# A decoder block on one core: ten up-projection pairs begun early, and down passes opened by four tiles with row buffers of their own

## The chip, the cores and the metric

The kernel runs on one core of one Trainium2 chip. The time is device microseconds (us) of one execution. Five engines matter here. TensorE (PE in the profile) multiplies matrices. VectorE (DVE) and ScalarE (ACT) do element-wise work. GpSimd (POOL) and SyncE (SP) do hardly anything here but issue transfers between the memory of the chip and the on-chip buffers. On ACT, DVE, POOL and SP the instructions of this trace start in the order of the engine's queue, so an instruction that waits holds up everything behind it on that engine, and a transfer that waits for its buffer holds up the transfers behind it in the same issuing queue.

## The reference

What is computed is one decoder block of 2048 channels over 512 tokens in float32. The first half (input projection, an RWKV-7 mixer, a pooling mixer) is not touched. The change lies in what follows it:

```python
mix = jnp.concatenate([y_rwkv, y_pool], axis=-1) @ w_out[l]      # 2048 -> 2048
x = x + gt1 * mix
h = _rmsnorm(x, norm2_g[l]) * (1.0 + sc2) + sh2
x = x + gt2 * _conv_ffn(h, w_up[l], conv_w[l], conv_b[l], w_down[l])
...
return _rmsnorm(x, norm_f_g)
```

`_conv_ffn` multiplies by `w_up` (2048 to 2 x 5632 columns, values and gates), convolves each column causally over three tokens, takes silu(gate) x value and multiplies by `w_down` (5632 to 2048). The two norms run over the 2048 channels of each token, so nothing of a token's second norm can be known before all sixteen output tiles of 128 channels have their values for that token.

## The kernel before

**Layout.** Channels lie on the 128 partitions, tokens along the free dimension. A tile `f` (0 to 15) is 128 channels by 512 tokens; `H0` and `H1` are the first and the second 256 tokens. Each float32 operand is split in a rounded part and a rest (`hi`, `lo`), and each product is three matmuls (`mm3`, L119 to L123). For weights ACT makes the rounded part (the cast of L837, or L114 in the output projection) and DVE the rest (L839, L116). The split weights have three buffers of each kind.

**Output projection** (L693 to L806). Tiles 0 to 7 are accumulated together in eight banks, tiles 8 and 9 (`NW = 10`) one after the other over all tokens, and tiles 10 to 15 first for `H0`, then for `H1`, as half tiles. `residual` (L734) adds a finished tile to `x` on DVE (L737), squares it on ACT (L731, into `sqx`) and adds the square to `acc` on DVE (L732). `out_done` stores the new `x` tile from SP (L764). During the last four half tiles the `H0` half is normed (`normed`, L779: one DVE multiply and four ACT instructions per four tiles) and split (`split4`, L786).

**Up projection.** The product with `w_up` is computed per pair j (0 to 43) of a value and a gate tile. It is one step of the Strassen-Winograd scheme: the tokens are cut in `H0` and `H1`, the channels in two halves, and each pair takes seven half-size products instead of eight. The operands on the side of `x` are Y11, Y21 (halves of `H0`) and T1 to T4, Y22 (sums that need `H1` as well). A product (`product`, L842) is 24 matmuls with 256 columns. The two rows of `w_up` of a pair (1 MB each) are loaded by SP (L852) into four buffers `x2_0` to `x2_3`, the ones that held `x` before; GpSimd adds to them in the transfer (L948 for r1, L951 for r3); DVE makes r2 and r4 (L972, L979). r2, r3, r4 and all other wide scratch, `sqx` among it, share one ring of three buffers, `wide` (L710).

The first two products of a pair need only `H0`. `first_two` (L859) makes them for `NB = 5` pairs before the loop and holds the sums in five of ten scratch buffers (`Slot`, L821; a list from which the longest free one is taken). Meanwhile `combos` (L871) norms the `H1` half and makes and splits T1 to T4 and Y22, one of four large steps after each pair. The loop over pairs (L941) then has five products for the first five pairs and seven for the other 39. The last product of pair j (`last_product`, L929) is issued in the iteration of pair j+1, and `finish_pair` (L914) convolves, multiplies and stores the result `ad` from SP (L924).

**Down projection** (L1008 to L1093). The 44 rows of `ad` are taken in two passes of 22. `act_pair` (L1008) loads them back through slots (`al`) and splits them. `down` (L1020) goes through one output tile in three blocks of up to eight rows, each with one weight transfer (L1024) into the `wide` ring. Pass one stores its sixteen partial tiles `yd` from SP (L1039). Pass two loads them and `x` (`load_x2`, L1054) from SP, adds tiles 0 to 7 over all tokens, then tiles 8 to 15 for `H0` and for `H1`, each followed by `residual`. The final norm of `H0` is written out (`finish`, L1068) between the last half tiles, that of `H1` at the end.

**Order.** Apart from a few marked places ahead of the change, no order is written by hand. A planner of the framework fixes each engine's queue before the run: the order of the program is the priority, and an instruction whose operands or whose buffer are not yet free by the planner's own estimates comes behind ready ones. Buffers of one ring are handed out in program order. At run time an instruction waits for its own operands and its own buffer, but never overtakes.

Of the kernel before, what the change touches and what calls it, by code (L numbers as in the profile page):

```python
# [9 lines left out]
F32 = mybir.dt.float32  # L10
# [6 lines left out]
P = 128  # L17
T = 512
D = 2048
KT = D // P  # L20
# [1 line left out]
NP = 8  # L22
NC = 4
WC = 512
NW = 10
NWF = 8
NSLOT = 10
NB = 5
NJ = NF // 2
Q = float(np.exp(-0.5))  # L30
WINS = (2, 4, 8, 16)
# [25 lines left out]
def block_kernel(ctx, tc, a, out, stop=None, dbg=None):  # L57
# [664 lines left out]
        return x2q[f // 4][:, f % 4, sl]  # L722

    acc = rb.tile([P, T], F32, tag="acc", name="acc")

    def sumsq(acc, src, lo, hi, fresh):
        if fresh:
            S.activation(acc[:, lo:hi], src, AF.Square)
        else:
            t = wide("sqx")[:, 0:2, :].rearrange("p a b -> p (a b)")  # L730
            S.activation(t[:, lo:hi], src, AF.Square)  # L731
            V.tensor_add(acc[:, lo:hi], acc[:, lo:hi], t[:, lo:hi])  # L732

    def residual(f, ps, gate, acc, lo, hi, fresh):  # L734

# [37 lines left out]
    def out_half(hf, f):  # L773
        ps = bank()[:, 0:HT]
# [41 lines left out]


    ub = ctx.enter_context(tc.tile_pool(name="ub", bufs=1, side="right", reuse_waits="tile"))
    free = [(ub, f"s{i}") for i in range(NSLOT)]

    class Slot:  # L821

# [31 lines left out]

    W1, W2 = slice(0, 2 * QW), slice(2 * QW, 4 * QW)
    T1, T2, T3, T4, Y22 = ([None, None] for _ in range(5))
    ahead = []

    def first_two(n):  # L859

        w = row(2 * n, ub, f"t4{n % 2}")
        s_ = Slot("u1")
        ps = bank()[:, 0:HT]
        product(ps, w[:, W1], Y11)
        S.copy(s_[:, H1], ps)
        ps = bank()[:, 0:HT]
        product(ps, w[:, W2], Y21)
        V.tensor_add(s_[:, H0], s_[:, H1], ps)
        ahead.append(s_)

    def combos(step):  # L871
        if step in (0, 1):
            normed(step, H1, rstd)
            t = wide("t1")
            V.tensor_sub(t, x2q[step][:, :, H0], x2q[step][:, :, H1])
            T1[step] = split4(ub, f"t1{step}", t)
        elif step in (2, 3):
            g = step - 2
            normed(g + 2, H1, rstd)
            t3 = wide("t3")  # L880
            V.tensor_sub(t3, x2q[g + 2][:, :, H1], x2q[g][:, :, H1])
            t2 = wide("t2")
            V.scalar_tensor_tensor(t2, t3, -1.0, x2q[g][:, :, H0], op0=ALU.mult, op1=ALU.subtract)
            T2[g] = split4(ub, f"t2{g}", t2)
            T3[g] = split4(ub, f"t3{g}", t3)
            Y22[g] = split4(ub, f"y22{g}", x2q[g + 2][:, :, H1])
# [3 lines left out]
    t4 = []  # L890
# [23 lines left out]
    def finish_pair(j, u1, u2):  # L914
        yv, yg = Slot("yv"), Slot("yg")
        conv(u1.t, yv.t, col("cw", j), col("cw", 88 + j), col("cw", 176 + j), col("cb", j))
        u1.done()

        conv(u2.t, yg.t, ncw[:, 0, j : j + 1], ncw[:, 1, j : j + 1], ncw[:, 2, j : j + 1], col("cb", 44 + j))
        u2.done()  # L920
        S.activation(yg.t, yg.t, AF.Silu)
        V.tensor_mul(yv.t, yv.t, yg.t)
        yg.done()
        nc.sync.dma_start(ad[j], yv.t)  # L924
        yv.done()

    pend = None
# [13 lines left out]
    for j in range(NF):  # L941
        w = []
        for i in range(2):
            w.append(row(2 * j + i, rb, f"x2_{rows % 4}"))
            rows += 1

        w11, w12, r1, w22 = w[0][:, W1], w[0][:, W2], w[1][:, W1], w[1][:, W2]
        G.dma_start(r1, a["wup"][2 * j + 1, :, W2], accum_op=ALU.add)  # L948
# [3 lines left out]
        early = j < NB  # L952
        pa = bank()[:, 0:HT]
        cap = Slot("cap")
        if early:
            u1 = ahead[j]
            if pend:
                last_product(pend)
        else:
            product(pa, w11, Y11)  # L960
            S.copy(cap[:, H0], pa)
            last_product(pend)
            u1 = Slot("u1")
            pb = bank()[:, 0:HT]
            product(pb, w12, Y21)
            V.tensor_add(u1[:, H0], cap[:, H0], pb)
# [3 lines left out]
        S.copy(cap[:, H1], pc)  # L970
        r2 = wide("r2").rearrange("p a b -> p (a b)")
        V.tensor_add(r2, r1, w11)  # L972
        product(pa, r2, T2, start=early)
        if early:
            V.tensor_add(cap[:, H0], u1[:, H1], pa)
        else:
            S.copy(cap[:, H0], pa)
# [1 line left out]
        V.tensor_add(r4, r2, w12)  # L979
        product(pc, r4, Y22, start=False)  # L980
        V.tensor_add(u1[:, H1], cap[:, H0], pc)
        if early:
# [46 lines left out]

    yd = [tc.dram_tile([P, T], F32, name=f"yd{f}") for f in range(KT)]  # L1030
    A = []
    for i in range(NJ // 2):
        A += act_pair(i)
    for f in range(KT):
        ps = bank()
        down(ps, f, 0, A)
        s_ = Slot("yd")
        S.copy(s_.t, ps)
# [13 lines left out]
    x2q = [quad(i, "x2") for i in range(4)]  # L1052

    def load_x2(f):  # L1054
        nc.sync.dma_start(x2(f), x2d[f])
        s_ = Slot("yd")
        nc.sync.dma_start(s_.t, yd[f])
        V.scalar_tensor_tensor(x2(f), s_.t, gate(f), x2(f), op0=ALU.mult, op1=ALU.add)
        s_.done()

# [10 lines left out]
        nc.sync.dma_start(out[:, k, hs], x2(k, hs))  # L1071

    for f in range(NWF):
        load_x2(f)
        load_x2(f + NWF)
        ps = bank()
        down(ps, f, 1, A)
        residual(f, ps, gate(f), acc, 0, T, f == 0)
    for f in range(NWF, KT):
        down_half(0, f)  # L1080
# [111 lines left out]
```

## Time and profile before

| | |
|---|---|
| median of 3 runs | 2539.76 us (2536.63 to 2545.37) |
| the profiled execution | 2535.93 us, of which the span is 2534.2 us |
| PE busy in the span | 2319.7 us (92%) |
| DVE, ACT, POOL busy | 1639.3, 1038.2, 78.8 us |
| mean granted TensorE clock | 0.974 |
| transfers | 470.44 MB, mean 186 GB/s |

The page divides the span in 40 slices of 63.4 us. The output projection lies in slices 13 to 16 (781 to 975 us), the early products and the pair loop from there to slice 31 (1915 us), pass one of the down projection to 2167 us and pass two to 2519 us. Transfers reach up to 365 GB/s in 10 us stretches. In the timelines of an engine a row is the start in us, the duration, the engine, the line, the operation, its result and operands, how many were merged, and in brackets the idle time before it with what ended it. A row that merges several shows their common duration.

### The profile page before, as it was taken

Reading aid. Unit: us, or ns where it says so; the run is one execution under the profiler, and the core shown is the slowest. Engines: PE = TensorE matmul, PEld = TensorE weight load, DVE = VectorE, ACT = ScalarE, POOL = GpSimd, SP = SyncE. Lnnn points to the kernel's source line nnn. Section 1 sums busy time; section 2 is a strip of 40 time slices with the busy share of each in tenths; the row PEclk is TensorE's granted clock in tenths of the full one; section 3 lists DMA queues with packets and bytes.
Section 4 is the critical chain, followed back from the end, with each engine's and each line's share of the span. In section 5 each row is a group of like instructions: output and inputs, shape, how many; then the busy total and the mean of one; then the engine's idle time right before and its main releaser. Section 6 shows DMA issues by size and latency. Waiting matters only on the chain.

```text
span 2534.2 us, 42335 instructions
## 1 busy us (share of the span) xinstructions
PE 2319.7 (92%) x17026; PEld 1998.0 (79%) x17026; DVE 1639.3 (65%) x2621; ACT 1038.2 (41%) x1466; POOL 78.8 (3%) x101
## 2 busy tenths in 40 slices
PE   4789999999999998689999999999998999988776
PEld 3556666666667898689999999999997888766765
DVE  7987777777854457677777777777777522522343
ACT  3243444444423347445555555555554222212222
POOL 0000000000000000100000000000000000000000
PEclk9999999999999999799999999999999999999988
DMA  9975565666636564777677766667778844523443
GB/s 350 344 223 145 152 183 148 181 174 180 180 106 192 157 181 152 216 204 196 194 203 201 199 193 190 193 196 204 200 207 296 302 146 138 168 69 92 114 148 108
DMA packets 215047, 470.44 MB, mean 186 GB/s; under 512 B 72961, under 2 KB 80065, under 8 KB 196033
## 3 DMA queue, kind: packets, MB, share of 16 engines
q1 hardware_dynamic: 202178, 421.59, 51.5%
q0 software_dynamic: 12672, 46.14, 10.6%
q8 instruction: 133, 2.18, 0.3%
q14 instruction: 64, 0.52, 0.1%
HBM read 431.74 MB, written 35.92 MB: 185 GB/s over the span
## 4 chain that ended last, share of the span: by engine, by line
PE 74%; DVE 11%; DMA 7%; issue 3%; ACT 3%; SPq 1%; POOL 0%; ACTq 0%; DVEq 0%; POOLq 0%
PE b L123 18%; PE b L121 18%; PE b L122 18%; PE mm L122 3%; PE mm L121 3%; PE mm L123 3%; DVE jk L213 3%; DMA wrow<-wup 2%; DVE ulo L839 2%; DMA war<-ada 1%; ACT uhi L837 1%; PE pb L538 1%; PE pb L536 1%; DMA al<-ad 1%; DMA wraw<-win 1%
## 5 line engine op out<-in xcount | busy, mean ns | idle before, releaser
L121 PE MATMUL b<-t,uhi 128*128 128x256 f32 x1408 | 401.3, 285 | 30.2 <-ACT uhi L837 28.4
L123 PE MATMUL b<-t,ulo 128*128 128x256 f32 x1408 | 401.0, 285 | 10.1 <-DVE ulo L839 10.1
L122 PE MATMUL b<-t,uhi 128*128 128x256 f32 x1408 | 400.5, 284 | 0.0
L121 PE MATMUL b<-act,uhi 128*128 128x512 f32 (+1 forms) x880 | 319.7, 363 | 58.4 <-ACT uhi L837 54.8
L123 PE MATMUL b<-act,ulo 128*128 128x512 f32 (+1 forms) x880 | 319.4, 363 | 15.9 <-DVE ulo L839 15.9
L122 PE MATMUL b<-act,uhi 128*128 128x512 f32 (+1 forms) x880 | 317.6, 361 | 0.4 <-DVE act L1016 0.4
L121 PE MATMUL b<-y,uhi 128*128 128x256 f32 x1056 | 297.7, 282 | 2.4 <-ACT uhi L837 2.4
L122 PE MATMUL b<-y,uhi 128*128 128x256 f32 x1056 | 298.7, 283 | 0.0
L123 PE MATMUL b<-y,ulo 128*128 128x256 f32 x1056 | 298.4, 283 | 0.0
L121 PEld LDWEIGHTS b<-t,uhi 128*128 128x128 f32 x1408 | 272.5, 194 | 31.6 <-ACT uhi L837 28.9
L837 ACT CAST uhi<-wrow 128x1024 fp32r<-128x1024 f32 x176 | 184.3, 1050 | 254.5 <-PE b L122 233.2
L123 PEld LDWEIGHTS b<-t,ulo 128*128 128x128 f32 x1408 | 272.3, 193 | 11.3 <-DVE ulo L839 11.3
L839 DVE TENSOR_TENSOR ulo<-wrow,uhi 128x1024 fp32r<-128x1024 f32 x176 | 215.2, 1224 | 97.5 <-ACT uhi L837 97.5
L122 PEld LDWEIGHTS b<-t,uhi 128*128 128x128 f32 x1408 | 272.2, 193 | 0.0
L114 ACT CAST whi<-wraw 128x512 fp32r<-128x512 f32 x228 | 140.7, 619 | 295.3 <-PE mm L122 125.4
L121 PEld LDWEIGHTS b<-act,uhi 128*128 128x128 f32 x880 | 175.1, 199 | 89.4 <-ACT uhi L837 61.2
L839 DVE TENSOR_TENSOR ulo<-wd,uhi 128x1024 fp32r<-128x1024 f32 (+1 forms) x120 | 134.2, 1135 | 167.3 <-ACT uhi L837 162.5
L116 DVE TENSOR_TENSOR wlo<-wraw,whi 128x512 fp32r<-128x512 f32 x228 | 156.0, 688 | 118.7 <-ACT whi L114 101.3
L123 PEld LDWEIGHTS b<-act,ulo 128*128 128x128 f32 x880 | 175.5, 199 | 45.3 <-DVE ulo L839 22.6
L837 ACT CAST uhi<-wd 128x1024 fp32r<-128x1024 f32 (+1 forms) x120 | 114.7, 973 | 219.5 <-PE b L122 170.0
L121 PEld LDWEIGHTS b<-y,uhi 128*128 128x128 f32 x1056 | 201.2, 191 | 2.8 <-ACT uhi L837 2.8
L837 ACT CAST uhi<-r 128x1024 fp32r<-128x1024 f32 x132 | 138.8, 1051 | 156.2 <-PE b L122 153.4
(302 smaller groups left out, 4629.5 us busy)
## 6 DMA issues: line engine op xcount, KB each, us to landing
wrow<-wup SPq DMA_DIRECT2D x93, 1024.0 KB, 4.8
wa<-ada SPq DMA_DIRECT2D x48, 1024.0 KB, 7.3
war<-ada SPq DMA_DIRECT2D x192, 256.0 KB, 3.6
wd<-wdn SPq DMA_DIRECT2D x80, 512.0 KB, 3.7
wraw<-win SPq DMA_DIRECT2D x140, 256.0 KB, 4.1
wraw<-wout SPq DMA_DIRECT2D x88, 256.0 KB, 3.5
r<-wup SPq DMA_DIRECT2D x44, 512.0 KB, 4.0
r<-wup POOLq DMA_DIRECT2D x44, 512.0 KB, 5.5
```

The costliest lines, as they stand in the source:

```text
L114: S.copy(hi, raw)
L116: eng.tensor_tensor(lo, raw, hi[:, :].bitcast(F32), op=ALU.subtract)
L121: PE.matmul(ps, wh, xh, start=start, stop=False, skip_group_check=more)
L122: PE.matmul(ps, wh, xl, start=False, stop=False, skip_group_check=more)
L123: return PE.matmul(ps, wl, xh, start=False, stop=stop, skip_group_check=more)
L213: V.scalar_tensor_tensor(jk, wa, 1.0, cb, op0=ALU.mult, op1=ALU.mult, accum_out=mod[:, j : j + 1])
L536: PE.matmul(pss[h][:, 0:128], bt[HS[h], cl], ar[HS[h], c, 1, :], start=True, stop=True)
L538: PE.matmul(pss[h][:, 128:384], kt[HS[h], cl], ar[HS[h], c, :, :], start=True, stop=True)
L837: S.copy(hi[:, 0:n], src)
L839: V.tensor_tensor(lo[:, 0:n], src, hi[:, 0:n].bitcast(F32), op=ALU.subtract)
```

## The change

The two constants change to `NB = 10` and `NSLOT = 6`, and `NW` goes. All of tiles 8 to 15 of the output projection become half tiles. The norm and split of `H0` become eight small steps handed out over the last six half tiles, those of `H1` and the sums twelve steps handed out over ten `first_two`. The sums of `first_two` are stored in memory and loaded back in the loop, so that `H0` and the first two products of ten pairs need six slots. The other 8 KB per partition make two row buffers, `wr`, which r3 and two of every five `w_down` blocks use in place of the `wide` ring. In the down passes `sqx` takes a slot. Each down pass opens with tiles 0 to 3 together, block by block. Stores of `x`, `ad`, `yd` and the loads of `x` and `yd` are issued from GpSimd instead of SP. The row buffers of the pairs are used in the order `x2_0`, `x2_2`, `x2_1`, `x2_3`.

```diff
-NW = 10
 NWF = 8
-NSLOT = 10
-NB = 5
+NSLOT = 6
+NB = 10
...
     acc = rb.tile([P, T], F32, tag="acc", name="acc")
+    free = []
 
     def sumsq(acc, src, lo, hi, fresh):
         if fresh:
             S.activation(acc[:, lo:hi], src, AF.Square)
         else:
-            t = wide("sqx")[:, 0:2, :].rearrange("p a b -> p (a b)")
+            s_ = Slot("sqx") if free else None
+            t = s_.t if s_ else wide("sqx")[:, 0:2, :].rearrange("p a b -> p (a b)")
             S.activation(t[:, lo:hi], src, AF.Square)
             V.tensor_add(acc[:, lo:hi], acc[:, lo:hi], t[:, lo:hi])
+            if s_:
+                s_.done()
...
-        nc.sync.dma_start(x2d[f][:, lo:hi], x2(f, slice(lo, hi)))
+        G.dma_start(x2d[f][:, lo:hi], x2(f, slice(lo, hi)))
...
-    for f in range(8, NW):
-        ps = bank()
-        project(ps, a["wout"][f, :, :], M)
-        out_done(f, ps, 0, T)
...
-    for f in range(NW, KT):
+
+    def first_half():
+        for q in (0, 1, 2, 3):
+            normed(q, H0, rstd)
+            yield
+            (Y11, Y21)[q // 2][q % 2] = split4(rb, f"y{q}", x2q[q][:, :, H0])
+            yield
+
+    for f in range(8, KT):
         out_half(0, f)
-    for f in range(NW, KT):
-        if f == NW + 1:
+    steps = first_half()
+    for f in range(8, KT):
+        if f == 9:
             dg = norm_rows(acc[:, H0])
-        if f == NW + 2:
+        if f == 10:
             rstd = norm_bcast(dg)
-        if f >= NW + 2:
-            n = f - NW - 2
-            q = (0, 2, 1, 3)[n]
-            normed(q, H0, rstd)
-            (Y11, Y21)[q // 2][q % 2] = split4(rb, f"y{q}", x2q[q][:, :, H0])
+        if f >= 10:
+            next(steps, None)
+            if f % 2:
+                next(steps, None)
         out_half(1, f)
...
-    ahead = []
+    early = [tc.dram_tile([P, T], F32, name=f"early{n}") for n in range(NB)]
...
-        ahead.append(s_)
-
-    def combos(step):
-        if step in (0, 1):
-            normed(step, H1, rstd)
+        G.dma_start(early[n], s_.t)
+        s_.done()
+
+    t4 = []
+
+    def combos():
+        for g in range(2):
+            normed(g, H1, rstd)
+            yield
             t = wide("t1")
-            V.tensor_sub(t, x2q[step][:, :, H0], x2q[step][:, :, H1])
-            T1[step] = split4(ub, f"t1{step}", t)
-        elif step in (2, 3):
-            g = step - 2
+            V.tensor_sub(t, x2q[g][:, :, H0], x2q[g][:, :, H1])
+            T1[g] = split4(ub, f"t1{g}", t)
+            yield
+        for g in range(2):
...
+    steps = combos()
     for n in range(NB):
         first_two(n)
         if n == 0:
             dg = norm_rows(acc[:, H1])
         if n == 1:
             rstd = norm_bcast(dg)
-        if 1 <= n < 5:
-            combos(n - 1)
+        if n >= 1:
+            next(steps, None)
+        if n in (2, 4, 6, 8):
+            next(steps, None)
+    for _ in steps:
+        pass
...
-        nc.sync.dma_start(ad[j], yv.t)
+        G.dma_start(ad[j], yv.t)
...
-            w.append(row(2 * j + i, rb, f"x2_{rows % 4}"))
+            w.append(row(2 * j + i, rb, f"x2_{(0, 2, 1, 3)[rows % 4]}"))
...
-        r3 = wide("r3").rearrange("p a b -> p (a b)")
+        r3 = ub.tile([P, 2 * QW], F32, tag="wr", name="r3", bufs=2)
...
-        if early:
-            u1 = ahead[j]
+        if j < NB:
+            u1 = Slot("u1")
+            G.dma_start(u1.t, early[j])
...
-    def down(ps, f, h, acts):
-        for k0 in range(0, NJ, 8):
+    nrow = [0]
+
+    def down_row():
+        nrow[0] += 1
+        if nrow[0] % 5 < 2:
+            return ub.tile([P, 2 * QW], F32, tag="wr", name="wd", bufs=2)
+        return wide("wd").rearrange("p a b -> p (a b)")
+
+    def down(ps, f, h, acts, blocks=(0, 8, 16)):
+        for k0 in blocks:
             n = min(8, NJ - k0)
-            w = wide("wd").rearrange("p a b -> p (a b)")
+            w = down_row()
...
+    def down_four(h, acts):
+
+        pss = [bank() for _ in range(4)]
+        for k0 in (0, 8, 16):
+            for f in range(4):
+                down(pss[f], f, h, acts, (k0,))
+        return pss
...
     for f in range(KT):
-        ps = bank()
-        down(ps, f, 0, A)
+        if f == 0:
+            pss = down_four(0, A)
+        ps = pss[f] if f < 4 else bank()
+        if f >= 4:
+            down(ps, f, 0, A)
...
-        nc.sync.dma_start(yd[f], s_.t)
+        G.dma_start(yd[f], s_.t)
...
-        nc.sync.dma_start(x2(f), x2d[f])
+        G.dma_start(x2(f), x2d[f])
         s_ = Slot("yd")
-        nc.sync.dma_start(s_.t, yd[f])
+        G.dma_start(s_.t, yd[f])
```

More of the change, by code (lines that the diff above doesn't have):

```diff
@@ L818, in block_kernel @@
     ub = ctx.enter_context(tc.tile_pool(name="ub", bufs=1, side="right", reuse_waits="tile"))
-    free = [(ub, f"s{i}") for i in range(NSLOT)]
+    free += [(ub, f"s{i}") for i in range(NSLOT)]
     class Slot:
@@ L868, in first_two @@
         V.tensor_add(s_[:, H0], s_[:, H1], ps)
-        ahead.append(s_)
-    def combos(step):
-        if step in (0, 1):
-            normed(step, H1, rstd)
+        G.dma_start(early[n], s_.t)
[5 more added lines that the diff above has]
+            yield
             t = wide("t1")
-            V.tensor_sub(t, x2q[step][:, :, H0], x2q[step][:, :, H1])
-            T1[step] = split4(ub, f"t1{step}", t)
-        elif step in (2, 3):
-            g = step - 2
+            V.tensor_sub(t, x2q[g][:, :, H0], x2q[g][:, :, H1])
+            T1[g] = split4(ub, f"t1{g}", t)
+            yield
+        for g in range(2):
             normed(g + 2, H1, rstd)
+            yield
             t3 = wide("t3")
@@ L883, in combos @@
             V.scalar_tensor_tensor(t2, t3, -1.0, x2q[g][:, :, H0], op0=ALU.mult, op1=ALU.subtract)
+            yield
             T2[g] = split4(ub, f"t2{g}", t2)
             T3[g] = split4(ub, f"t3{g}", t3)
+            yield
             Y22[g] = split4(ub, f"y22{g}", x2q[g + 2][:, :, H1])
@@ L888, in combos @@
             t4.append(t2)
-    t4 = []
+            yield
+    steps = combos()
     for n in range(NB):
@@ L948, in block_kernel @@
         G.dma_start(r1, a["wup"][2 * j + 1, :, W2], accum_op=ALU.add)
-        r3 = wide("r3").rearrange("p a b -> p (a b)")
+        r3 = ub.tile([P, 2 * QW], F32, tag="wr", name="r3", bufs=2)
         nc.sync.dma_start(r3, a["wup"][2 * j, :, W1])
         G.dma_start(r3, a["wup"][2 * j + 1, :, W1], accum_op=ALU.add)
-        early = j < NB
         pa = bank()[:, 0:HT]
         cap = Slot("cap")
-        if early:
-            u1 = ahead[j]
+        if j < NB:
+            u1 = Slot("u1")
+            G.dma_start(u1.t, early[j])
             if pend:
@@ L972, in block_kernel @@
         V.tensor_add(r2, r1, w11)
-        product(pa, r2, T2, start=early)
-        if early:
+        product(pa, r2, T2, start=j < NB)
+        if j < NB:
             V.tensor_add(cap[:, H0], u1[:, H1], pa)
@@ L981, in block_kernel @@
         V.tensor_add(u1[:, H1], cap[:, H0], pc)
-        if early:
+        if j < NB:
             pd = bank()[:, 0:HT]
@@ L1073, in block_kernel @@
     for f in range(NWF):
+        if f == 0:
+            pss = down_four(1, A)
         load_x2(f)
         load_x2(f + NWF)
-        ps = bank()
-        down(ps, f, 1, A)
+        ps = pss[f] if f < 4 else bank()
+        if f >= 4:
+            down(ps, f, 1, A)
         residual(f, ps, gate(f), acc, 0, T, f == 0)
```

## The prediction

> **What bounds the kernel now.** I read the page first, then busy time in stretches of 10 us and more, then the timelines of ACT, DVE, SP and POOL where PE is not full. The page and the stretches:
>
> ```profile
> PE 2319.7 (92%) x17026; PEld 1998.0 (79%) x17026; DVE 1639.3 (65%) x2621; ACT 1038.2 (41%) x1466; POOL 78.8 (3%) x101
> ...
> 1200.00:1880.00 680.00, 680.00 (x5673) 680.00 (x5672) 512.62 (x574) 355.62 (x473) 57.82 (x67) 1.00 0.70 197
> ...
> 910.00:920.00 10.00, 10.00 (x86) 10.00 (x85) 5.99 (x11) 5.04 (x9) 0.00 (x0) 1.00 0.66 196
> ...
> 1010.00:1020.00 10.00, 0.00 (x0) 0.00 (x0) 8.99 (x9) 5.95 (x8) 0.00 (x0) 0.56 0.74 258
> ...
> 2260.00:2440.00 180.00, 143.76 (x859) 127.89 (x860) 61.12 (x78) 43.15 (x54) 0.00 (x0) 0.92 0.36 103
> ```
>
> PE bounds the whole only on average. In the pair loop (1200 to 1880) it is full at clock 1.00; nothing there can be won but by fewer matmuls, and the change takes none away. Around 1010 it does nothing while DVE is full. From 2260 on it is busy 80% with DVE at 34%, ACT at 24%, transfers at 36%: nothing is full, so an order or a latency binds. These two places are what the change can win.
>
> **Prices of PE work.** They come from stretches in which PE is full:
>
> ```profile
> 1302.55 0.42 DVE L981 TENSOR_TENSOR u<-cap,b 128x256 f32<-128x256 f32 x1 [0.76 <-PE b L123]
> ...
> 1322.69 0.42 DVE L981 TENSOR_TENSOR u<-cap,b 128x256 f32<-128x256 f32 x1 [0.76 <-PE b L123]
> ...
> 1954.46 0.58 ACT L1038 COPY yd<-b 128x512 f32<-128x512 f32 x1
> ...
> 1969.64 0.58 ACT L1038 COPY yd<-b 128x512 f32<-128x512 f32 x1
> ```
>
> A pair of seven products takes 20.14 us, so a product 2.877 us and a 256-column matmul 0.120 us. A full down tile takes 15.18 us (66 matmuls of 0.230 us). A half down tile has 66 x 0.120 = 7.9 us of work, a half output tile (48) 5.75 us.
>
> **Part 1, pass two of the down projection: `sqx` out of the `wide` ring, five row buffers.**
>
> ```profile
> 2166.89 0.58 ACT L1038 COPY yd<-b 128x512 f32<-128x512 f32 x1
> ...
> 2239.36 0.75 DVE L737 SCALAR_TENSOR_TENSOR x<-b,mod,x 128x512 f32<-128x512 f32 x1 [13.10 <-PE b L123]
> ...
> 2240.20 0.63 ACT L731 ACTIVATE sqx<-x 128x512 f32<-128x512 f32 x1 [14.94 <-DVE x L737]
> ...
> 2240.74 1.98 ACT L837 CAST uhi<-wd 128x1024 fp32r<-128x1024 f32 x2
> ...
> 2259.72 0.75 DVE L737 SCALAR_TENSOR_TENSOR x<-b,mod,x 128x512 f32<-128x512 f32 x1 [13.12 <-PE b L123]
> ...
> 2345.23 0.48 DVE L737 SCALAR_TENSOR_TENSOR x<-b,mod,x 128x256 f32<-128x256 f32 x1 [4.65 <-PE b L123]
> ...
> 2369.13 0.48 DVE L737 SCALAR_TENSOR_TENSOR x<-b,mod,x 128x256 f32<-128x256 f32 x1 [4.68 <-PE b L123]
> ...
> 2436.27 5.96 DVE L1070 SCALAR_TENSOR_TENSOR x<-x,vec,b 128x256 f32<-128x256 f32 x15
> ...
> 2519.23 0.48 DVE L737 SCALAR_TENSOR_TENSOR x<-b,mod,x 128x256 f32<-128x256 f32 x1 [4.64 <-PE b L123]
> ```
>
> A full tile takes 20.36 us in place of 15.18, two half tiles 23.90 in place of 15.8. ACT stands 14.94 us before the square of the tile that PE is still making, and right behind it come the casts of the next tile's weights: two at once, already loaded. So ACT and DVE queues have the residual ahead of the next weights, and PE runs dry at each tile's end. I put this down to the ring: `sqx` is handed out of `wide` between the blocks of tile f and those of f+1, so the planner has no buffer for f+1's first block until the square is planned. Two rows speak for that. In pass one, where blocks alone use the ring, a tile takes 15.18 us; and in the output projection, with the same `residual` but weights in rings of their own, PE is full (910 to 920).
>
> The pass takes 2519.23 - 2166.89 = 352.3 us for 8 x 15.18 + 16 x 7.9 = 248 us of work. With `sqx` in a slot I expect 254: work, some 3 us at the start (below) and 3 us where 15 writes of `finish` stand ahead of splits (5.96 us now). Gain 98 us; bounds 104 (no loss left) and 84 (0.5 us at each of 19 tiles, and 6 + 5 us at the two places).
>
> **Part 2, opening passes with four tiles.** Pass one opens like this:
>
> ```profile
> 1915.29 0.37 ACT L934 COPY u<-b 128x256 f32<-128x256 f32 x1
> ...
> 1928.37 0.62 ACT L1015 CAST act<-al 128x512 fp32r<-128x512 f32 x1 [2.82 <-DMA al<-ad]
> ...
> 1940.46 0.58 ACT L1038 COPY yd<-b 128x512 f32<-128x512 f32 x1
> ...
> ad<-yv SPq DMA_DIRECT2D x44, 256.0 KB, 2.0
> ...
> al<-ad SPq DMA_DIRECT2D x44, 256.0 KB, 4.1
> ```
>
> The first tile ends 25.2 us after the last product, 10 us over its work, for it needs all 22 rows of `ad`. Four tiles need 12 blocks but only eight rows for the first 4 x 5.5 us, so the 10 us should go. But the slot list, counted through by hand, has seven entries now instead of eleven, and the last pair's u1, u2, yg, yv go to rows 3 to 6 where they went to rows 7 to 10. Row 6 waits for the store of yv (2.0 us) and its own load (4.1 us), and is cast at about 1928 as now; all four tiles need it in their first block. I expect 7 of the 10 us to stay. Gain 3 (bounds 8, if the planner lets tiles 1 and 2 run while row 6 is out, and -1). At pass two the same list gives row 6 the slot of tile 15's `yd`; hence the 3 us in part 1.
>
> **Part 3, ten early pairs, spread sums.**
>
> ```profile
> 975.26 0.48 DVE L737 SCALAR_TENSOR_TENSOR x<-b,mod,x 128x256 f32<-128x256 f32 x1 [0.50 <-PE b L123]
> ...
> 1009.59 0.42 DVE L868 TENSOR_TENSOR u<-u,b 128x256 f32<-128x256 f32 x1
> ...
> 1018.97 1.22 DVE L790 TENSOR_TENSOR y<-x,y 128x1024 fp32r<-128x1024 f32 x1
> 1020.11 1.22 DVE L790 TENSOR_TENSOR t<-t,t 128x1024 fp32r<-128x1024 f32 x1
> ...
> 1034.90 1.22 DVE L972 TENSOR_TENSOR r<-wrow 128x1024 f32<-128x1024 f32 x1 [9.98 <-DMA wrow<-wup]
> ...
> 1085.25 2.13 SPq L852 DMA_DIRECT2D wrow<-wup  x2
> ...
> 1090.61 0.86 POOL L948 DMA_DIRECT2D wrow<-wup  x1 [14.09 <-DMA wrow<-wup]
> ...
> 1099.54 1.23 DVE L972 TENSOR_TENSOR r<-wrow 128x1024 f32<-128x1024 f32 x1 [4.11 <-issue]
> ...
> 1104.66 2.13 SPq L852 DMA_DIRECT2D wrow<-wup  x2
> ...
> wrow<-wup POOLq DMA_DIRECT2D x44, 512.0 KB, 5.6
> ```
>
> Now: from the last output tile (975.26) to the last product (1915.29) are 940.0 us; 39 pairs of 20.14 take 785.5, which leaves 154.5 for 35 products (100.7 us of work). 54 us are lost: 3 before the first product, some 27 between the last early sum (1009.59) and the first pair, whose rows can be loaded only once DVE is through with `x` (r2 added at 1034.90), and 24 in the first five pairs.
>
> After: 34 pairs and 70 products. The 3 us stay. While 20 products run (57.5 us of PE) (their rows, five of 1 MB more than now, need 182 GB/s) DVE has 20 weight rests, 8 splits, 8 sums and 4 norm multiplies at 1.14 us (1018.97 to 1020.11) and 10 adds of 0.42, together 50 us: hidden, but with 13% to spare, so I put 6 us (0 to 14). The first pair's buffers are free four `first_two` before the loop, so its 27 us go; 4 us (0 to 8) for transfers crowding there. In the early pairs a circle of waits sets the pace: rows loaded (1085.25), r1 added in the transfer (1090.61), r2 added (1099.54), then the split that frees the next rows (1104.66): 19.4 us for 14.4 us of PE. r1's transfer took 8.9 us there, next to r3's, against 5.6 in the middle; r3 has its own two buffers now and can go earlier (-3.3), the loading back of u1 adds 256 KB, 0.9 us at 281 GB/s (197 at a share of 0.70). That gives 17.0 us. Bounds: 19.4, and 14.9, which 4096 KB per early pair need at 281 GB/s. The first two pairs have their rows; 8 x 2.6 = 21. Lost then 3 + 6 + 4 + 21 = 34, gain 20; bounds 54 - 9 = 45, and 54 - (3 + 14 + 3 + 50) = -16.
>
> **Part 4, output projection.** It takes 96.8 us now (rows 878.46 and 975.26):
>
> ```profile
> 878.46 0.75 DVE L737 SCALAR_TENSOR_TENSOR x<-pa,mod,x 128x512 f32<-128x512 f32 x1 [0.52 <-PE pa L123]
> ```
>
> Work is 96 x 0.230 + 12 x 5.75 = 91 us; after, 16 x 5.75 = 92. Tiles 8 and 9 load and split their weights twice (eight more of 256 KB); DVE, at 60% there, has room. The steps are spread over six tiles instead of four, which should leave 1 to 2 of the 5.7 us of stalls. Gain 3 (5 to -1).
>
> **Part 5, transfers moved to POOL.** 116 issues move from SP (44 `ad`, 24 `x`, 16 `yd`, 32 loads) and 20 are new, at 0.86 us each, beside PE; SP's own queue loses the waits of those stores, which cost nothing in the loop. POOL's queue is then what can be late: the `ad` store waits for the product of DVE, and r1's transfer may stand behind it.
>
> ```profile
> 1309.94 0.86 POOL L948 DMA_DIRECT2D wrow<-wup  x1 [11.39 <-DMA wrow<-wup]
> ...
> 1316.13 0.68 DVE L922 TENSOR_TENSOR yv<-yv,yg 128x512 f32<-128x512 f32 x1
> ...
> 1328.31 1.05 ACT L837 CAST uhi<-wrow 128x1024 fp32r<-128x1024 f32 x1 [1.81 <-PE b L122]
> ...
> L948 POOL DMA_DIRECT2D wrow<-wup x44: 862/862/881, 1025.8 to 1874.2; - x44
> ```
>
> Behind a store issued at 1316.8, r1's transfer would start at 1317.7 and land at 1323.3; its cast comes at 1328.31. 5 us are left, so I take 0 (bounds 0 and 0.5 us in each of 34 pairs, 17). The Trainium skill (DMA: Bandwidth & Descriptors, "SWDGE vs HWDGE vs iDMA") speaks against the move: GpSimd writes its descriptors into on-chip memory from which VectorE can lock it out, while SyncE's transfers are immune. By that rule each issue could stretch; in this trace it does not (862 to 881 ns over 44 issues, with DVE at 75%). Were each r1 issue of ten early pairs held for one DVE instruction of 1.22 us, the sum would be 12 us higher, 2424.
>
> **Sum.** -98 - 3 - 20 - 3 = -124. Against the profiled execution (2535.93 us: span 2534.2 and 1.7 around it; 0.15% under the median of 2539.76) that is 2412 us. All gains at their best give 2374, all at their worst with the 17 us 2487.
>
> **Rivals.** (a) *The order stays.* If the planner keeps the residual ahead of the casts for another reason (PE's last matmul being later in its plan than in fact), part 1 gives nothing: 2412 + 98 = 2510. Against it stand pass one and the output projection; 8%. (b) *The early pairs are bound by transfers.* Ten at 19.4 us and a tight DVE before them: part 3 costs 16 instead of gaining 20, 2448. The circle of waits is not cut by the change, which speaks for it; 15%. (c) *Slower: POOL's queue holds up r1.* The price is 34 us for every us by which r1's cast is late in a pair; the 124 us are gone at 3.7 us, that is when r1's transfer goes out 16 us later than at 1309.94. With 5 us of lateness it is 2412 + 170 = 2582. It takes a store that waits for the next iteration's product; 5%. (d) Part 1 works and all else cancels to no change at all: 2%.
>
> **Numbers.** The forecast has 70%: 2412 with 2385 to 2435 around it. The range must take in (b), not (a): 2385 to 2460. A change within 0.3% (7.6 us) could not be told from none. Faster 0.93 (forecast, (a), (b)), same 0.02 (d), slower 0.05 (c).
>
> **What would show it.** In pass two, residuals 15.2 and 7.9 us apart, and no wait of ACT for L737 over 8 us; PE idle around 1010 gone, ten L868 rows 5.8 us apart; early pairs 17 us apart at r2's add; a first `yd` copy some 68 us after the last product, the next three close behind; pairs still 20.14 us apart. The forecast is wrong if casts still follow the squares, or if the pairs in the middle are more than 20.2 us apart.

## The result and the profile after

The changed kernel takes 2608.59 us (median of 4 runs, 2601.99 to 2615.64) against 2542.05 us (4 runs): 1.026 times the time before, interval 1.023 to 1.030. Slower was the side to which I had given 5%; the forecast was 2412 us, so I was wrong. The profiled execution took 2610.18 us (span 2608.1, clock 0.961).

The page after, from its parts 1, 4 and 6 (the last column of part 6 is the median time from issue to landing):

```profile
PE 2357.0 (90%) x17122; PEld 2042.6 (78%) x17122; DVE 1641.9 (63%) x2648; ACT 1037.5 (40%) x1466; POOL 153.9 (6%) x237
...
DMA wrow<-wup 14%; PE b L120 9%; PE b L121 9%; PE b L122 9%; ACT uhi L844 2%; DVE ulo L846 2%; DVE yg L929 1%; DMA al<-ad 1%; ACT cap L989 0%; DMA yd<-yd 0%; DVE u L985 0%; DVE x L1108 0%; DMA ad<-yv 0%; SPq L1033 0%; DVE yv L941 0%
...
wrow<-wup SPq DMA_DIRECT2D x98, 1024.0 KB, 7.2
...
r<-wup POOLq DMA_DIRECT2D x44, 512.0 KB, 9.2
```

The same two transfers before:

```profile
wrow<-wup SPq DMA_DIRECT2D x93, 1024.0 KB, 4.8
...
r<-wup POOLq DMA_DIRECT2D x44, 512.0 KB, 5.5
```

The page names the new bound: the chain that ended last now goes through the rows of `w_up` (14% of the span, 2% before), and these two transfers of the pair loop take half as long again or more. The stages, from the timelines of DVE (L740 is `residual`, L875 the sum of `first_two`, L955 the last product of an early pair, L985 the second product of a later one) and ACT (L1076 copies a tile of pass one, L1034 casts a row of `ad`):

```profile
947.45 0.48 DVE L740 SCALAR_TENSOR_TENSOR x<-b,mod,x 128x256 f32<-128x256 f32 x1
...
957.05 0.48 DVE L740 SCALAR_TENSOR_TENSOR x<-b,mod,x 128x256 f32<-128x256 f32 x1 [0.73 <-PE b L122]
...
984.17 0.48 DVE L740 SCALAR_TENSOR_TENSOR x<-b,mod,x 128x256 f32<-128x256 f32 x1 [3.05 <-PE b L122]
...
994.28 0.42 DVE L875 TENSOR_TENSOR u<-u,b 128x256 f32<-128x256 f32 x1 [0.52 <-PE b L122]
...
1057.47 0.42 DVE L875 TENSOR_TENSOR u<-u,b 128x256 f32<-128x256 f32 x1 [4.83 <-issue]
...
1072.56 0.42 DVE L955 TENSOR_TENSOR u<-cap,b 128x256 f32<-128x256 f32 x1 [1.41 <-PE b L122]
...
1255.41 0.42 DVE L955 TENSOR_TENSOR u<-cap,b 128x256 f32<-128x256 f32 x1 [0.36 <-PE b L122]
...
1266.99 0.41 DVE L985 TENSOR_TENSOR u<-cap,b 128x256 f32<-128x256 f32 x1
...
2072.07 0.42 DVE L985 TENSOR_TENSOR u<-cap,b 128x256 f32<-128x256 f32 x1
...
2141.03 0.58 ACT L1076 COPY yd<-b 128x512 f32<-128x512 f32 x1
...
2153.26 0.58 ACT L1076 COPY yd<-b 128x512 f32<-128x512 f32 x1
...
2335.56 0.58 ACT L1076 COPY yd<-b 128x512 f32<-128x512 f32 x1
...
2348.59 0.62 ACT L1034 CAST act<-al 128x512 fp32r<-128x512 f32 x1 [8.36 <-DMA al<-ad]
...
2405.19 0.75 DVE L740 SCALAR_TENSOR_TENSOR x<-b,mod,x 128x512 f32<-128x512 f32 x1 [1.35 <-PE b L122]
...
2420.37 0.75 DVE L740 SCALAR_TENSOR_TENSOR x<-b,mod,x 128x512 f32<-128x512 f32 x1 [1.97 <-PE b L122]
...
2593.35 0.48 DVE L740 SCALAR_TENSOR_TENSOR x<-b,mod,x 128x256 f32<-128x256 f32 x1 [5.87 <-PE b L122]
```

| stretch | before | forecast | after |
|---|---|---|---|
| up to output tile 7 (unchanged code) | 878.5 | 878.5 | 882.1 |
| output projection | 96.8 | 93.8 | 102.1 |
| last output tile to last product (2088.18) | 940.0 | 920 | 1104.0 |
| pass one | 251.6 | 248.6 | 247.4 |
| pass two | 352.3 | 254 | 257.8 |

The 94.5 us of pass two are there. They are lost again, with 70 more, in the middle: 33 intervals between 34 later pairs take (2072.07 - 1266.99) / 33 = 24.40 us each where 20.14 was the price of the matmuls, 141 us in all, and the ten early pairs come 20.3 us apart. Who waits there, from the list of waits between 1200 and 2080 us (total, times, longest):

```profile
ACT yg L940 <- DVE yg L929: 200.2, 35, 7.9
...
DVE r L991 <- DMA wrow<-wup: 167.5, 36, 6.9
```

Before, between 1140 and 1910 us, ACT's SiLU had waited for DVE once, for 0.9 us, and DVE's r2 add never for a transfer. One pair of the loop, from the timelines of SP, POOL, DVE and ACT:

```profile
1546.28 3.27 SPq L859 DMA_DIRECT2D wrow<-wup  x2
...
1546.09 0.86 POOL L970 DMA_DIRECT2D r<-wup  x1 [5.73 <-DMA r<-wup]
1552.40 0.85 POOL L967 DMA_DIRECT2D wrow<-wup  x1 [5.45 <-DVE ulo L846]
...
1554.80 0.75 DVE L928 SCALAR_TENSOR_TENSOR yg<-u,ncw,yg 128x511 f32<-128x511 f32 x1
1560.69 1.22 DVE L991 TENSOR_TENSOR r<-wrow 128x1024 f32<-128x1024 f32 x1 [5.14 <-DMA wrow<-wup]
1561.83 0.74 DVE L929 SCALAR_TENSOR_TENSOR yg<-u,ncw,yg 128x510 f32<-128x510 f32 x1
...
1562.67 0.63 ACT L940 ACTIVATE yg<-yg 128x512 f32<-128x512 f32 x1 [6.17 <-DVE yg L929]
1563.20 1.03 ACT L844 CAST uhi<-r 128x1024 fp32r<-128x1024 f32 x1
1564.14 0.36 ACT L989 COPY cap<-b 128x256 f32<-128x256 f32 x1
...
1570.95 1.23 DVE L846 TENSOR_TENSOR ulo<-wrow,uhi 128x1024 fp32r<-128x1024 f32 x1 [0.38 <-ACT uhi L844]
...
1572.20 3.57 SPq L859 DMA_DIRECT2D wrow<-wup  x2
```

Read it as a circle. A split frees a row buffer and SP loads the next pair's rows (1546.28). When they are in, GpSimd issues r1's adding transfer (1552.40), 6.1 us later. r2's add on DVE needs r1 (1560.69), 8.3 us later. Behind r2's add in DVE's queue stands the *second tap of `yg`*, which belongs to an earlier pair and needs only the first tap (1554.80); behind that tap waits the SiLU on ACT; behind the SiLU stand a cast of the next weights and the copy of L989, which empties the bank that PE's product with r4 adds to. PE waits for that copy, and the split that frees the next row comes at 1570.95. Around once: 25.9 us. The page's row of these matmuls (idle time before them and what ended it) and busy time in two stretches of this pair (PE, PEld, DVE, ACT, POOL, then granted clock, transfer share and GB/s):

```profile
L120 PE MATMUL b<-y,uhi 128*128 128x256 f32 x1056 | 323.4, 306 | 97.7 <-ACT cap L989 95.3
...
1546.00:1561.00 15.00, 15.00 (x127) 15.00 (x126) 6.59 (x9) 5.56 (x7) 1.70 (x2) 1.00 0.79 211
1561.00:1572.00 11.00, 7.74 (x43) 7.53 (x42) 8.52 (x10) 4.82 (x7) 1.13 (x2) 0.69 0.23 72
```

So the wait costs twice. PE stands idle for some 3 us, and the matmuls after the pause run at a lower clock: 43 in 7.74 us of busy time, at a mean clock of 0.69 in these 11 us, where 127 had taken 15.00 at 1.00. Between 1266.99 and 2072.07 PE is busy 712.8 of 805.1 us. That makes 92 of the 141 us idle time; by my estimate the other 48 or so go with the clock, whose mean is 0.93 there.

The order before was another in these pairs:

```profile
1313.22 0.74 DVE L909 SCALAR_TENSOR_TENSOR yg<-u,ncw,yg 128x511 f32<-128x511 f32 x1
1314.00 0.75 DVE L910 SCALAR_TENSOR_TENSOR yg<-u,ncw,yg 128x510 f32<-128x510 f32 x1
...
1316.73 1.22 DVE L972 TENSOR_TENSOR r<-wrow 128x1024 f32<-128x1024 f32 x1
```

There both taps and the product of `yv` (1316.13) stand ahead of r2's add, so r1 could be late without anyone but r2 noticing. From this I formed three theories. **O**: the order, r2's add four places too early (ahead of the tap, an add, a weight rest and the product of `yv`). **T**: the transfers, r3's being no longer held back by the ring and running against the row load (1546.09 and 1546.28). **P**, my rival (c): GpSimd's queue.

### The profile page after: what moved, and what is told of

It reads as the page before. It is cut to its first block, busy times and chain, and to the rows that moved or that the text cites. A ratio compares the mean times of both kernels' runs of the same rounds, so it can differ in the third digit from the quotient of the medians.

```text
span 2608.1 us, 42719 instructions
## 1 busy us (share of the span) xinstructions
PE 2357.0 (90%) x17122; PEld 2042.6 (78%) x17122; DVE 1641.9 (63%) x2648; ACT 1037.5 (40%) x1466; POOL 153.9 (6%) x237
## 4 chain that ended last, share of the span: by engine, by line
PE 27%; DMA 15%; issue 4%; DVE 4%; ACT 3%; SPq 0%; POOL 0%; ACTq 0%; POOLq 0%; DVEq 0%
DMA wrow<-wup 14%; PE b L120 9%; PE b L121 9%; PE b L122 9%; ACT uhi L844 2%; DVE ulo L846 2%; DVE yg L929 1%; DMA al<-ad 1%; ACT cap L989 0%; DMA yd<-yd 0%; DVE u L985 0%; DVE x L1108 0%; DMA ad<-yv 0%; SPq L1033 0%; DVE yv L941 0%
## 5 line engine op out<-in xcount | busy, mean ns | idle before, releaser
L120 PE MATMUL b<-y,uhi 128*128 128x256 f32 x1056 | 323.4, 306 | 97.7 <-ACT cap L989 95.3
L122 PE MATMUL b<-y,ulo 128*128 128x256 f32 x1056 | 319.0, 303 | 2.2 <-DVE ulo L846 2.2
L121 PE MATMUL b<-y,uhi 128*128 128x256 f32 x1056 | 319.5, 303 | 0.0
L120 PE MATMUL b<-act,uhi 128*128 128x512 f32 (+1 forms) x880 | 307.4, 350 | 9.6 <-ACT act L1034 8.6
L121 PE MATMUL b<-act,uhi 128*128 128x512 f32 (+1 forms) x880 | 307.5, 350 | 0.5 <-DVE act L1035 0.5
L122 PE MATMUL b<-act,ulo 128*128 128x512 f32 (+1 forms) x880 | 307.4, 350 | 0.0
L120 PEld LDWEIGHTS b<-y,uhi 128*128 128x128 f32 x1056 | 222.9, 211 | 104.8 <-ACT cap L989 102.0
L120 PEld LDWEIGHTS b<-t,uhi 128*128 128x128 f32 x1408 | 276.6, 197 | 12.2 <-ACT uhi L844 10.3
L121 PEld LDWEIGHTS b<-t,uhi 128*128 128x128 f32 x1408 | 275.5, 196 | 0.0
L115 DVE TENSOR_TENSOR wlo<-wraw,whi 128x512 fp32r<-128x512 f32 x236 | 161.6, 688 | 118.5 <-ACT whi L113 105.7
L122 PEld LDWEIGHTS b<-y,ulo 128*128 128x128 f32 x1056 | 221.6, 210 | 2.6 <-DVE ulo L846 2.6
L121 PEld LDWEIGHTS b<-y,uhi 128*128 128x128 f32 x1056 | 222.1, 210 | 0.0
L846 DVE TENSOR_TENSOR ulo<-r,uhi 128x1024 fp32r<-128x1024 f32 x132 | 161.2, 1222 | 59.7 <-ACT uhi L844 59.7
```

The source lines that it names most:

```text
L115: eng.tensor_tensor(lo, raw, hi[:, :].bitcast(F32), op=ALU.subtract)
L120: PE.matmul(ps, wh, xh, start=start, stop=False, skip_group_check=more)
L121: PE.matmul(ps, wh, xl, start=False, stop=False, skip_group_check=more)
L122: return PE.matmul(ps, wl, xh, start=False, stop=stop, skip_group_check=more)
L846: V.tensor_tensor(lo[:, 0:n], src, hi[:, 0:n].bitcast(F32), op=ALU.subtract)
```

## The experiments

Each ratio is against runs of the kernel before on the same chip, with its interval. A "pair" is the mean distance of the L985 rows (or of their counterpart) behind the early pairs.

**e1_r3_wide: r3 back in the ring.**

```diff
-        r3 = ub.tile([P, 2 * QW], F32, tag="wr", name="r3", bufs=2)
+        r3 = wide("r3").rearrange("p a b -> p (a b)")
```

> The changed kernel with r3 back in the wide ring, nothing else. The planned DVE queue then has r2's add behind the product of yv and yg again. Theory O (r3's own buffers let the planner put r2's add ahead of the second yg tap, so that SiLU and the next weights' casts wait for r1's transfer): the pairs after the first ten go from 24.4 us apart to 20.1, which is 33 x 4.26 = 141 us, so about 2468 (2450 to 2480). Theory T (r3's transfers, no longer held back by the ring, run against the row load and make r1 late): the same, since the ring holds them back again; this run does not part O from T. Theory P (POOL's queue: the store of ad or r3's transfer stands ahead of r1's): POOL carries the same issues as in the changed kernel, so pairs stay near 24.4 us and the time near 2608.

2449.66 us, 0.959 (0.954 to 0.963); a pair 20.15 us. The one line that gives r3 its own buffers carries the loss of the middle. POOL still makes all its issues, though r1's now stands ahead of r3's; that speaks against P, and e3 and e10 settle it. O and T are left.

**e2_pin_r2: r3 keeps its buffers, r2's add goes back to its place.**

```diff
-        V.tensor_mul(yv.t, yv.t, yg.t)
+        muls.append(V.tensor_mul(yv.t, yv.t, yg.t))
...
+    muls = []
...
-        V.tensor_add(r2, r1, w11)
+        if len(muls) > 1:
+            with tc.issue_after(muls[-2].ins):
+                V.tensor_add(r2, r1, w11)
+        else:
+            V.tensor_add(r2, r1, w11)
```

> The changed kernel with r3 in its own two buffers as there, but r2's add tied behind the product of yv and yg of the pair two before, so that the planned queues of DVE and ACT in the loop are those of the kernel before; SP's and POOL's are those of the changed kernel. Theory O: pairs 20.1 us apart, about 2468 (2450 to 2480). Theory T: r1 still lands 8 to 9 us after its issue beside r3's transfers; r2's add, and the split of r2 behind it, wait for it wherever they stand, so pairs stay over 22 us apart and the time over 2540. Theory P: 24.4 us and 2608.

2434.63 us, 0.954 (0.949 to 0.958): with e7 below, which is built on it, the fastest of all, ahead of both kernels. A pair takes 20.20 us. The timelines of POOL and DVE, and the rows that give the distances (L956 and L986 are L955 and L985 here):

```profile
1073.02 0.42 DVE L956 TENSOR_TENSOR u<-cap,b 128x256 f32<-128x256 f32 x1 [1.40 <-PE b L122]
...
1226.46 0.42 DVE L956 TENSOR_TENSOR u<-cap,b 128x256 f32<-128x256 f32 x1 [0.64 <-PE b L122]
...
1230.01 0.42 DVE L986 TENSOR_TENSOR u<-cap,b 128x256 f32<-128x256 f32 x1
...
1508.96 0.85 POOL L968 DMA_DIRECT2D wrow<-wup  x1 [4.71 <-DMA wrow<-wup]
...
1513.72 0.69 DVE L941 TENSOR_TENSOR yv<-yv,yg 128x512 f32<-128x512 f32 x1
1516.42 1.23 DVE L994 TENSOR_TENSOR r<-wrow 128x1024 f32<-128x1024 f32 x1 [2.00 <-DMA wrow<-wup]
...
1896.54 0.42 DVE L986 TENSOR_TENSOR u<-cap,b 128x256 f32<-128x256 f32 x1
```

r1 still takes 7.5 us and DVE still waits 2.0 us for it, but with the tap and the product done ahead nobody pays. The early pairs come 17.05 us apart. T alone falls.

**e3_ad_sp: the store of `ad` back on SP.**

```diff
-        G.dma_start(ad[j], yv.t)
+        nc.sync.dma_start(ad[j], yv.t)
```

> The changed kernel with only the store of ad back on SP's queue. Theory P in the form in which I had it as rival (c) (the store waits for the product and r1's transfer stands behind it): pairs 20.1 us apart, about 2468. Theories O and T: DVE's order and r3's transfers are unchanged, so pairs stay 24.4 us apart within 0.5 us, 2590 to 2620.

2604.78 us, 1.020 (1.013 to 1.027); a pair 24.46 us. P falls in the form of rival (c). Its other form, that r3's transfer holds up r1's in POOL's queue, falls with e10.

**e8_no_r3_add: the bad order, without r3's adding transfer.**

```diff
-        G.dma_start(r3, a["wup"][2 * j + 1, :, W1], accum_op=ALU.add)
```

> The changed kernel as it is, with the order in which r2's add stands ahead of the second yg tap, but r3's adding transfer left out (512 KB less per pair; r3 is then one of its two terms only, so the last products are computed from another operand). The queues of DVE and ACT are planned the same. If the time of a pair is the circle through the row load and r1's transfer, it falls with these two: in the changed kernel 6.1 and 8.3 us, here about 5 and 6.5, so 21 to 22.5 us per pair and 2500 to 2545 in all. If the order alone costs 4.3 us whatever the transfers take, pairs stay 24.4 us apart and the time near 2605.

2443.60 us, 0.959 (0.950 to 0.968); a pair 20.33 us. I had expected 21 to 22.5: the order alone costs next to nothing. So O alone falls too, and a new theory **C** says that it takes both: r2's add ahead of the tap *and* r1 landing late.

**e9_one_buf: one buffer for r3 instead of two**, to move r3's transfers away in time with all computed.

```diff
-        r3 = ub.tile([P, 2 * QW], F32, tag="wr", name="r3", bufs=2)
+        r3 = ub.tile([P, 2 * QW], F32, tag="wr", name="r3", bufs=1)
...
-        if nrow[0] % 5 < 2:
-            return ub.tile([P, 2 * QW], F32, tag="wr", name="wd", bufs=2)
+        if nrow[0] % 5 < 1:
+            return ub.tile([P, 2 * QW], F32, tag="wr", name="wd", bufs=1)
```

> The changed kernel with one buffer instead of two in the ring that r3 and two of the five down rows use; all is still computed, and the planned order of DVE, ACT, SP and POOL in the loop is that of the changed kernel, r2's add ahead of the second yg tap included. r3's load now waits until the last r3 is split, so it moves away from the row load and r1's transfer. Theory C (order and crowded transfers together: with r3's adding transfer left out pairs were 20.3 us apart): the row load and r1's transfer come back to about 5 and 5.6 us and pairs fall to 20.1 to 21.5 us, 2460 to 2520. If the order alone, or something else that leaving the transfer out also removed, made the 24.4 us: 24.4 us and 2600 or more. If r1's transfer is held up behind r3's in POOL's queue, pairs are longer still, over 24.4 us.

2602.82 us, 1.021 (1.009 to 1.033); a pair 24.41 us. This run misses its aim. The timelines of POOL and SP show that r3's transfers did not move:

```profile
1507.98 0.86 POOL L970 DMA_DIRECT2D r<-wup  x1 [5.59 <-DMA r<-wup]
...
1508.31 3.27 SPq L859 DMA_DIRECT2D wrow<-wup  x2
```

The one buffer had been free in time, so the second is worth nothing in the loop, and C is not tested.

**e10_narrow_add: the same issues and waits as the changed kernel, an eighth of the bytes.**

```diff
-        G.dma_start(r3, a["wup"][2 * j + 1, :, W1], accum_op=ALU.add)
+        G.dma_start(r3[:, 0:P], a["wup"][2 * j + 1, :, 0:P], accum_op=ALU.add)
```

> The changed kernel with r3's adding transfer narrowed to the first 128 of its 1024 columns (64 KB instead of 512; r3 is then wrong in the other 896 columns, everything else is computed). Issues, their order in POOL's and SP's queues, waits and the order on DVE and ACT are all those of the changed kernel; only the bytes go. If the bytes make the row load and r1's transfer late (theory C), these come back to about 5 and 5.6 us and pairs are 20.2 to 20.6 us apart, 2440 to 2455, as with the transfer left out. If it was the issue on POOL, or the wait of that issue for r3's load with r1's issue behind it, pairs stay 24.4 us apart and the time near 2605.

2450.38 us, 0.958 (0.946 to 0.970); a pair 20.48 us. Once around the circle, from the timelines of SP, POOL and DVE:

```profile
1512.07 3.27 SPq L859 DMA_DIRECT2D wrow<-wup  x2
...
1517.96 0.85 POOL L967 DMA_DIRECT2D wrow<-wup  x1 [3.26 <-DVE ulo L846]
...
1523.38 1.23 DVE L991 TENSOR_TENSOR r<-wrow 128x1024 f32<-128x1024 f32 x1 [2.04 <-DMA wrow<-wup]
...
1532.65 3.27 SPq L859 DMA_DIRECT2D wrow<-wup  x2
```

r1 takes 5.4 us instead of 8.3 and the circle 20.6 us, just over PE's 20.14. It is the bytes, not the issue or its wait. Between 1300 and 1900 us PE waits for the copy of L989 11 times, at most 1.6 us, and the clock stays 1.00; in the changed kernel it waits 24 times there, up to 3.9 us, and the clock is 0.93. The four cases of C:

| pair, us | r2's add ahead of the tap | behind tap and product |
|---|---|---|
| r3's transfer beside the row load | 24.40 (changed kernel) | 20.20 (e2) |
| gone, small, or held back by the ring | 20.33 (e8), 20.48 (e10) | 20.15 (e1) |

The Trainium skill (DMA: Bandwidth & Descriptors, "Queues, rings and completion order") says that each transfer engine takes turns between the queues that have work for it. That agrees with a load of 1 MB and an adding transfer of 512 KB landing in 7.2 and 9.2 us side by side, against 4.8 and 5.5 us before. The mean share of the transfers fell meanwhile: between 1300 and 1900 us it is 0.58 after, where it had been 0.70.

The early pairs bear C out. They come 20.3 us apart in the changed kernel, 17.8 in e8 and 17.6 in e10. In e1 they are still 19.2 us apart: r1's transfers land in 7.7 us in the median there (1070 to 1210 us), and r2's add stands ahead of the second tap in most of them. In e2 the transfers land in the same 7.7 us, the order is mended, and they come 17.05 us apart.

**e4_sqx_slot: the kernel before with only `sqx` moved.**

```diff
-            t = wide("sqx")[:, 0:2, :].rearrange("p a b -> p (a b)")
+            s_ = Slot("sqx") if free else None
+            t = s_.t if s_ else wide("sqx")[:, 0:2, :].rearrange("p a b -> p (a b)")
...
+            if s_:
+                s_.done()
```

> The kernel before with one edit: sqx goes into a slot in pass two instead of the wide ring; four row buffers as before. Part 1's mechanism (the ring hands sqx out between the blocks and so puts the residual ahead of the next casts): pass two falls from 352 us to some 254, in all about -95 us, 2445 (2435 to 2460). If instead the fifth row buffer made the gain, the pass stays near 352 us and the time near 2540; in between, both did.

2442.47 us, 0.956 (0.951 to 0.961). The last copy of pass one on ACT and the residuals on DVE:

```profile
2181.05 0.58 ACT L1042 COPY yd<-b 128x512 f32<-128x512 f32 x1
...
2212.68 0.75 DVE L741 SCALAR_TENSOR_TENSOR x<-b,mod,x 128x512 f32<-128x512 f32 x1 [1.97 <-PE b L123]
...
2227.85 0.75 DVE L741 SCALAR_TENSOR_TENSOR x<-b,mod,x 128x512 f32<-128x512 f32 x1 [1.97 <-PE b L123]
...
2431.18 0.48 DVE L741 SCALAR_TENSOR_TENSOR x<-b,mod,x 128x256 f32<-128x256 f32 x1 [5.87 <-PE b L123]
```

Pass two takes 250.1 us with the three row buffers of the `wide` ring (the expectation says four, but the ring has three, and the changed kernel had five with `wr`): the two more are not needed, and all other parts of the change are worth 8 us together even when the order is mended, which is no part of the change (2434.63 on the same chip). The granted clock over pass two is 1.00, where it had been 0.92 before: there too, part of the loss had been clock.

**e5_nb5: e2 with five early pairs.**

```diff
-NB = 10
+NB = 5
```

> The run with r2's add tied (2434 us, early pairs 17.05 us apart), with NB back at 5: five early pairs instead of ten. Part 3's value alone. If the ten early pairs hide what they were meant to hide, the stretch from the last output tile to the last product goes from 927.8 us back to about the 943 us that the kernel before needed on this chip, so 2450 (2443 to 2458). If the early pairs' own circle of waits takes the gain back (rival b of the prediction), the stretch stays within 4 us and the time at 2434.

2442.26 us, 0.959 (0.953 to 0.964). The middle takes 937.8 us against 927.8 with ten (928.2 and 928.3 in e6 and e7 on this chip): five more early pairs are worth 10 us, less than the 15 expected.

**e6_plain_open2: e2, pass two opened tile by tile.**

```diff
-        if f == 0:
-            pss = down_four(1, A)
...
-        ps = pss[f] if f < 4 else bank()
-        if f >= 4:
-            down(ps, f, 1, A)
+        ps = bank()
+        down(ps, f, 1, A)
```

> The run with r2's add tied, with pass two opened tile by tile again; pass one keeps its four tiles. Pass two took 257.8 us with the four tiles there and 250.1 us in the kernel before with sqx in a slot. If the four tiles lose the 8 us (all four wait for the row of ad that comes last), the pass falls to about 250 and the time to 2427. If it is the late row itself (the slot of the last yd, whose store on POOL went out 4.2 us after its copy, behind loads of yd), a first tile by itself waits for it as well, and the pass stays at 256 to 260 and the time at 2434.

2436.35 us, 0.956 (0.950 to 0.962); pass two takes 262.1 us, 4.3 more than with four tiles and over the 256 to 260 expected. So the four tiles are not the cost. The first tile ends 28.4 us after the last copy of pass one, for 15.2 us of work: it waits for all 22 rows, the last of them cast 25.3 us after that copy. The four tiles hide part of this.

**e7_yd_sp: e2, the store of `yd` on SP.**

```diff
-        G.dma_start(yd[f], s_.t)
+        nc.sync.dma_start(yd[f], s_.t)
```

> The run with r2's add tied, with the store of yd back on SP's queue, four tiles at both openings. If the late row comes from POOL's queue (store at 2164.03, copy done at 2160.40, load of the row at 2169.28, cast at 2173.76), the row comes some 4 us earlier and pass two takes about 254 us, as I had predicted: 2430. If the row is late for other reasons, 257.8 us and 2434.

2433.99 us, 0.956 (0.949 to 0.963); pass two takes 254.8 us against 257.8 (257.4 in e5 on this chip), the late row is cast 3.3 us earlier relative to the last copy (10.6 us behind it instead of 13.9). The stage shows it; in the whole time, 2433.99 and 2434.63 in two sets of runs, it can't be told.

## Why the prediction was wrong

The step that failed is the price of the 34 pairs in the middle. **Part 3** put them at 20.14 us because PE was full there, and counted "r3 has its own two buffers now and can go earlier" as a gain of 3.3 us for the early pairs alone. **Part 5** looked at what the moved stores do to r1, found 5 us to spare up to r1's cast and took 0. But r1's cast is not the first to read r1: in the kernel before r2's add on DVE reads it at 1316.73, 11.6 us ahead of the cast, and nothing was set down for a wait there. Both parts took the order of DVE's queue as given and asked only when a transfer starts. (My test for it was the right one: pairs more than 20.2 us apart.) But the planner orders a queue by when it believes buffers to be free: with r3 out of the ring, it put r2's add ahead of the second tap in the later pairs as well. It had stood there before in three of the five early pairs. The prediction shows one of these (r2's add at 1099.54), and the second tap comes behind it in the timeline of DVE:

```profile
1100.68 0.74 DVE L910 SCALAR_TENSOR_TENSOR yg<-u,ncw,yg 128x510 f32<-128x510 f32 x1
```

That pair takes 19.4 us. The prediction read a circle of transfers there, not an order. What was off:

- *The loop*, +141 us against a bound of 17. My 5 us were the time up to r1's own cast, in the old order. In the new one the lateness of r1 goes by r2's add to SiLU, the copy of L989 and PE, and with PE's pauses its clock falls. Rival (c) had the sign and the thing that comes late, r1, but not the place: e3 and e10 show that it is not POOL's queue. My text itself held the rule that I needed, since in part 1 the order of ACT and DVE hung on which buffers the ring hands out; I applied it to `sqx` and not to r3.
- *The early pairs*: 20.3 us instead of 17.0, by the same circle. In e2 they take 17.05 us, but that the number is met is luck: the working had r1's transfer 3.3 us faster, at 5.6 us, and in e2 it still lands in 7.7 us there. The order made the gain, and the prediction had not counted it.
- *Early sums*: ten L875 rows lie 7.0 us apart (63.2 / 9), not 5.8. DVE is busy 50.3 us of these 63.2, as planned. The first nine rows are 6.4 us apart; before the tenth (1045.45 to 1057.47) 12.0 us pass. PE waits 4.8 of them, up to 1049.16, at the first matmul of the first pair's r1 product, which stands in its queue ahead of the rest of the early products. That matmul's cast (1048.07) had waited for r1's transfer (issued at 1037.72, landed 10.3 us later), and the clock behind it is 0.64 (1050 to 1057). With e2 the middle is 927.8 us against 920: part 3 gains about 12 us, not 20.
- *Part 1*: -94.5 us against -98, and its mechanism stands alone in e4. Residuals come 15.2 and 7.9 us apart. "Five row buffers" was no part of it.
- *Part 2*: the first copy comes 52.9 us after the last product, where I had said some 68, and the fourth 65.1 after it (the 68 hold the work of all four tiles, but the first is done three blocks earlier); pass one gains 4.2 us, predicted 3. At pass two I had counted 3 us at the start; the late row costs 8.9 (2405.19 - 2335.56 - 60.7), 3 of them by the `yd` store that waits on GpSimd's queue (e7). That is a cost of part 5 that I had at 0.
- *Part 4*: +5.3 us instead of -3. Tiles with two steps still stall (947.45 to 957.05 is 9.6 us for 5.75 us of work), twice.
- *Part 5 on the lock-out*: the issues of r1 stay at 851 ns each in the median (848 to 900), so the Trainium skill's warning of a lock-out by VectorE (DMA: Bandwidth & Descriptors, "SWDGE vs HWDGE vs iDMA") does not show, as before.
- *The range*: the lower bound of part 3 adds 3 us for transfers crowding where the text has up to 8; with 8 it is -21, and the worst sum 2492 instead of 2487. The result lies far outside of both.

Against the forecast the profiled execution is 198 us longer: 184 in the middle, 8 in the output projection, 4 in pass two, 4 in code that did not change, -1 in pass one. e2 gets 176 of the 198 back by moving one instruction per pair, in the early pairs too; of the 22 that stay, 8 lie in the middle.

## What to carry to other kernels

When a change gives a buffer its own ring, compare each engine's queue before and after around every instruction that waits for a transfer: a planner moves what has become free, and in an in-order queue a waiting add ahead of a ready one hands its lateness to everybody behind it. A full engine gives the price of a loop only as long as every circle (buffer free, load, second transfer, add, split, buffer free) is shorter than its work; add it up in the trace and ask what each edit does to it. Where one part of a change carries nearly all the gain, run it alone: one small edit to the kernel before gave 115 of the 123 us that the best version gave beside it.

## What was unexpected of the hardware

Two causes that each cost at most 0.35 us per pair cost 4.3 us together (20.20, and 20.33 to 20.48, against 24.40). Part of that is the clock: a pause of PE costs more than its length where the clock falls with it (0.69 between 1561 and 1572 us of the changed kernel, with 3.3 us idle), while the pauses of at most 1.6 us in e10 leave it at 1.00. And transfers can bind while their mean share falls: r1's adding transfer of 512 KB lands in 7.6 us in the median of the changed kernel and in 5.7 us in e10, where the other adding transfer carries an eighth of the bytes.
